# Second token group's v units by seven block products with transposes, ahead of the attention

## The chip, the cores and the metric

The kernel runs on one core of a Trainium2 chip. The time is in device microseconds (us), the median of the runs shown; the profile is one further execution on the same kind of chip. The engines are named as in the profile: PE (TensorE, matmuls), PEld (its weight loads), DVE (VectorE), ACT (ScalarE), POOL (GpSimd) and SP (SyncE, which here only issues DMAs).

## The reference

One encoder layer over 1280 tokens (1024 of a prompt, 256 of a sample), model width 2048, everything float32:

```
hn   = rmsnorm(x, norm_w)
proj = einsum('btd,dp->btp', hn, w_in)        # 2048 -> 9232 columns
na_q, na_k, na_v, na_g, ml_qk, ml_v, ml_o, ml_z, ml_gp = split(proj)
att  = neighbourhood_attention(na_q, na_k, na_v, na_rpb)   # 8 heads of 128
att  = att * silu(na_g)
qk   = silu(centred_depthwise_conv(ml_qk)); mq, mk = split(qk)
h    = bidirectional_mlstm(mq, mk, ml_v, gates)            # 4 heads of 256
mem  = rmsnorm(h) * sigmoid(ml_o) * silu(ml_z)
y    = rmsnorm(x + concat(att, mem) @ w_out)
```

The change touches only how the columns na_v and ml_v of `proj` are computed for some of the tokens.

## The kernel before

Every float32 operand of a large matmul is split into a high and a low half (ACT copies the high half, DVE subtracts to get the low one), and each product is the sum of three matmuls. The 1280 tokens go in two groups: 768 (group one, `GA`) and 512 (group two, `GB`). The projection's columns go in units of 256: `n1` counts columns in steps of 128, q from 0, k from 8, g from 16, conv (ml_qk) from 24, o from 40, z from 48, and eight v units from `NCH` = 56, of which v units 0 to 3 serve attention heads two by two and v units 4 to 7 serve one mLSTM head each.

The program has four stages.

- **Group one** (`first_tiles`, `unit_vg`, `pair_a`): every unit by seven products of half-size blocks in place of eight (a Strassen scheme). Four of its weight sums, `SUMS` = 6, 5, 7, 3, are written to DRAM (`sD`, line 590) for each unit in the table `SECOND`.
- **Group two, ahead of the attention**: v units 4 and 0 and one q unit plainly (`proj_v`, `proj_pair`), then each unit of `SECOND` by seven products (`pair_s`, matmuls of 256 columns, tiles named `S<n1>...`), reading the stored sums back. `finish_s` finishes a unit while the next one's products run.
- **The attention and the mLSTM** (`run` over two streams of steps; tiles `nas`, `nap` for the attention, `mls`, `mlp` for the mLSTM). The remaining units of group two are written in the program ahead of it, at lower priority, so that a planner with a simulated clock lays them between the attention's instructions on each engine: `proj_v` (tiles `pv`, `wsv`) for v units 1, 2, 3, 5, 6, 7, `proj_pair` (tiles `pc`, `ws`, `pco`) for nine pairs of q and conv columns and, last of all, eight pairs of o and z columns in `late_gate`. In this document these are called the fillers.
- **The output projection** (`product`, tiles `mb`, `mo`, `wo`, `po`): 14 block products. Its operand blocks `mb` are read back from DRAM by DMAs that POOL issues; their tiles lie in memory that the attention's pool (`att_ctx`) gives up.

A plain v unit is 4 token tiles x 16 slices of the model width x 3 matmuls = 192 matmuls of 256 columns; a plain pair is 96 matmuls of 512 columns; a unit by seven products is 7 x 8 x 3 = 168 matmuls of 256 columns.

All engines run their instructions in the order that the planner has set; an instruction waits for its semaphores and holds up what is behind it on its engine. So PE takes an attention matmul only where the order has it, and an engine can run ahead only as far as the tiles' buffers allow (for example one `npt` buffer, three `nst`, eight `hf`, five PSUM banks of tag "a").

Of the kernel before, what the change touches and what calls it, by code (L numbers as in the profile page):

```python
# [10 lines left out]
F32R = mybir.dt.float32r  # L11
# [3 lines left out]
P = 128  # L15
# [5 lines left out]
GA, GB = 768, 512  # L21
GSZ, GOF = (GA, GB), (0, GA)
NA_H, ML_H = 8, 4
EPS = 1e-6
NEG = -1.0e30
NCH = 56
# [3 lines left out]
NRA, NWS, NWT, NPC, NPO = 3, 8, 4, 5, 6  # L30
# [9 lines left out]
SECOND = (  # L40
    GT0, QK0 + 8, GT0 + 2, QK0, KT0, GT0 + 4, KT0 + 2, GT0 + 6, KT0 + 4,
    KT0 + 6,
)
LATE = (0, 2, 4, 6)
SUMS = (6, 5, 7, 3)

# [2 lines left out]
def kernel(  # L49
# [18 lines left out]
    V, S, G, PE, DM = nc.vector, nc.scalar, nc.gpsimd, nc.tensor, nc.sync  # L68
# [5 lines left out]
    def f(ap):  # L74
        return ap.bitcast(F32)

    def bank(tag, name):
        return ps.tile([P, 512], F32, tag=tag, name=name, bufs=3 if tag == "pr" else 5)
# [19 lines left out]
    ident = const.tile([P, P], F32, tag="ident", name="ident")  # L98
# [78 lines left out]
    def split(hi, lo, src, scale=None):  # L177
        if scale is None:
            S.copy(hi, src)  # L179
            return V.tensor_tensor(lo, src, f(hi), op=ALU.subtract)  # L180
        else:
            S.mul(hi, src, scale)
            return V.scalar_tensor_tensor(lo, src, scale, f(hi), op0=ALU.mult, op1=ALU.subtract)
# [30 lines left out]
    def store_qk(n, C, new, parts):  # L214
        hi, lo = new(F32R), new(F32)
        for c0, w, row in parts:
            cs = slice(c0, c0 + w)
            if row is None:
                split(hi[:, cs], lo[:, cs], C[:, cs])
            elif n < KT0:  # L220
                split(q_view(hi[:, cs]), q_view(lo[:, cs]), q_rows(C[:, cs]))
            else:
                split(k_view(hi[:, cs]), k_view(lo[:, cs]), k_rows(C[:, cs]))
        if n < KT0:
            store_q(n, (f(hi), lo), parts)
            return
        w = sum(w for _, w, _ in parts)
        t0 = 0 if w == GA else GA
        for z, t in enumerate((f(hi), lo)):
            DM.dma_start(kS[n - KT0][:, z, t0 : t0 + w], t[:, :w])  # L230
# [4 lines left out]
    def store_v(u, t0, o, src, scale=None):  # L235
        if u >= NA_H // 2:
            hi, lo = o[:, 0], o[:, 1]
        else:
            hi, lo = (o.rearrange("p a (j d) -> p (a j) d", j=2).rearrange(
                "p (j z) d -> p z j d", z=2)[:, z] for z in range(2))  # L240
            src = src.rearrange("p (j d) -> p j d", j=2)
        split(hi, lo, src, scale)
        flat = f(o).rearrange("p a d -> p (a d)")
        if u >= NA_H // 2 or t0 >= TP:
            DM.dma_start(vS[u][t0 : t0 + P], flat)
            return
        dst = vS[u][t0 // 256 * 256 : t0 // 256 * 256 + 256].rearrange("(c r) x -> r c x", r=4)
        for r in range(2):
            DM.dma_start(dst[t0 % 256 // 64 + r], flat[64 * r : 64 * r + 64])
# [397 lines left out]
    wb, xp0 = pools  # L647
# [9 lines left out]
    def po(name):  # L657
        return wb.tile([P, 520], F32, tag="po", name=name, bufs=NPO)
# [15 lines left out]
    def conv_b(o, ct):  # L674
        cv = po(f"pcv{ct}")
        yield from conv_taps(cv, o, ct, 516, 0)
        hi = wb.tile([P, 520], F32R, tag="po", name=f"pch{ct}", bufs=NPO)
        store_conv(ct, cv, hi, o, ((0, 258, GA - 2), (260, 516, TP)))
# [700 lines left out]
    def pair_s(n1, tag, bg):  # L1379
# [63 lines left out]
        for o, c in zip(Cn, ((c0, c1), (c2, c3))):  # L1443
# [3 lines left out]
            else:  # L1447
                out_scaled(o[:, :GB], o[:, :GB], rbs[1], n1)
        return finish_s(n1, Cn)

    def finish_s(n1, Cn):
        for j, o in enumerate(Cn):
            if QK0 <= n1 < OT0:
                ct = n1 - QK0 + j
                DM.dma_start(o[:, 0:4], qb[ct])
                for z in (260, 518):
                    G.memset(o[:, z : z + 2], 0.0)
                yield from conv_b(o, ct)
                continue
            o = o[:, :GB]  # L1460
            if n1 < GT0:
                store_qk(
                    n1 + j, o,
                    lambda dt: wb.tile([P, 520], dt, tag="po", name=f"S{n1}_{j}_{dt}", bufs=NPO),
                    PARTS_B,
                )
                yield
                continue
            if OT0 <= n1 < ZT0:
                S.activation(o, o, AF.Tanh, scale=0.5)  # L1470
            elif n1 >= GT0:
                th = po(f"S{n1}th{j}")[:, :GB]
                S.activation(th, o, AF.Tanh, scale=0.5)
                V.scalar_tensor_tensor(o, th, 1.0, o, op0=ALU.add, op1=ALU.mult)
            DM.dma_start(pT[n1 + j][:, GA:], o)
            yield
# [16 lines left out]
    for i in range(ML_H):  # L1493
        for u in (("v", 4 + i), QK0 + 8 + 2 * i, QK0 + 2 * i, ("v", i), QT0 + 2 * i, KT0 + 2 * i):
            if isinstance(u, tuple):
                if i:
                    proj_v(u[1], X)
            elif u not in SECOND and u != QT0:
                proj_pair(u, X)
# [368 lines left out]
```

## Time and profile before

| | us |
|---|---|
| median of 3 runs | 2542.15 (2541.53 to 2543.43) |
| span of the profiled execution | 2540.0 |
| PE busy | 2523.1 |
| DVE busy | 1980.9 |
| ACT busy | 1348.3 |
| POOL busy | 597.7 |

The profiled execution's own time is its span of 2540.0 us, 2.15 us under the median of the runs. "Busy" on PE counts a matmul from its start to its modelled end, and neighbours overlap, so a busy PE is not a PE at its peak; the number of matmuls in a stretch of time tells more. Group one ends at about 1089 us, the units of `SECOND` at 1362 us, the last attention matmul at 2100 us, and the output projection starts at 2143 us.

### The profile page before, as it was taken

The numbers are of one execution on the slowest core, as the hardware profiler recorded it, in microseconds if no ns is written. First come the engines' busy times: TensorE is split into PE (matmuls) and PEld (weight loads), VectorE is DVE, ScalarE is ACT, GpSimd is POOL, SyncE is SP. The second block draws the span as 40 slices with busy tenths as digits, with TensorE's granted clock in tenths as the row PEclk, the third lists the DMA queues.
The fourth block names the chain that finished last, engine by engine and source line by source line (L and its number), as shares of the span: only waits on it lengthen the run. The fifth ranks groups of instructions, "written<-read, shape, count | busy, mean of one in ns | idle before, by whom it ended". The sixth has DMA issues, their size and how long they took to land.

```text
span 2540.0 us, 44864 instructions
## 1 busy us (share of the span) xinstructions
PE 2523.1 (99%) x15197; PEld 2363.7 (93%) x15197; DVE 1980.9 (78%) x4034; ACT 1348.3 (53%) x3052; POOL 597.7 (24%) x883
## 2 busy tenths in 40 slices
PE   9999999999999999999999999999999999999998
PEld 9999999999999999999999899899998888888887
DVE  8787878898879798898875676775875665889696
ACT  8644455444444444475655666666665653344445
POOL 0553555544444454400000011010100103000002
PEclk9999999999999999999999999999999999999999
DMA  6563464546434342467778878878977849546327
GB/s 218 171 206 122 140 215 146 183 130 201 152 112 130 100 140 89 151 229 221 230 249 279 263 265 290 284 252 274 300 219 246 287 125 355 198 146 208 95 87 257
DMA packets 308189, 505.67 MB, mean 199 GB/s; under 512 B 49040, under 2 KB 195000, under 8 KB 307960
## 3 DMA queue, kind: packets, MB, share of 16 engines
q1 hardware_dynamic: 304856, 490.75, 60.0%
q0 software_dynamic: 2960, 11.80, 1.2%
q8 instruction: 120, 1.97, 0.3%
q14 instruction: 109, 0.89, 0.1%
q10 hardware_dynamic: 144, 0.26, 0.0%
HBM read 374.18 MB, written 128.52 MB: 198 GB/s over the span
## 4 chain that ended last, share of the span: by engine, by line
PE 87%; DMA 2%; DVE 2%; issue 0%; ACT 0%; POOL 0%; SPq 0%; POOLq 0%; ACTq 0%; DVEq 0%
PE pc L694 16%; PE po L1684 15%; PE pv L777 5%; PE A22b L288 1%; PE A44b L288 1%; PE A14b L288 1%; PE A18b L288 1%; PE A10b L288 1%; PE A48b L288 1%; PE A52b L288 1%; PE A50b L288 1%; PE A42b L288 1%; PE A20b L288 1%; PE A16b L288 1%; PE A12b L288 1%; PE A70b L288 1%
## 5 line engine op out<-in xcount | busy, mean ns | idle before, releaser
L1684 PE MATMUL po<-wo,mo 128*128 128x512 f32 (+1 forms) x1620 | 374.2, 392 | 0.0
L1684 PEld LDWEIGHTS po<-wo,mo 128*128 128x128 f32 x1620 | 303.3, 188 | 70.1
L180 DVE TENSOR_TENSOR ws<-wr,ws 128x512 fp32r<-128x512 f32 x144 | 97.9, 690 | 40.4 <-ACT ws L179 38.0
L179 ACT CAST ws<-wr 128x512 fp32r<-128x512 f32 x144 | 87.5, 617 | 64.9 <-PE pc L694 56.3
L179 ACT CAST mo<-mb 128x640 fp32r<-128x640 f32 x72 | 52.0, 726 | 108.8 <-PE po L1684 96.2
L120 POOL TENSOR_SCALAR rs<-rs 128x1 f32<-128x1 f32 x9 | 4.2, 468 | 370.4 <-DVE rs L1637 367.2
L180 DVE TENSOR_TENSOR mo<-mb,mo 128x640 fp32r<-128x640 f32 x72 | 58.4, 817 | 32.2 <-ACT mo L179 32.1
L1605 DVE TENSOR_TENSOR y<-y,po 128x512 f32<-128x512 f32 x89 | 57.2, 680 | 13.5 <-PE po L1684 13.3
L179 ACT CAST mo<-ms 128x640 fp32r<-128x640 f32 x40 | 28.9, 725 | 51.9 <-PE po L1684 30.6
L180 DVE TENSOR_TENSOR wsv<-wr_v,wsv 128x512 fp32r<-128x512 f32 x64 | 44.6, 702 | 12.5 <-ACT wsv L179 12.2
L179 ACT CAST wsv<-wr_v 128x512 fp32r<-128x512 f32 x64 | 38.9, 616 | 23.1 <-PE pv L777 13.5
L430 DVE SCALAR_TENSOR_TENSOR pcv<-pco,cw_sb,pcv 128x516 f32<-128x516 f32 x48 | 36.1, 753 | 7.7 <-ACT pcv L424 7.7
L180 DVE TENSOR_TENSOR mo<-ms,mo 128x640 fp32r<-128x640 f32 x40 | 32.7, 816 | 10.7 <-ACT mo L179 10.7
L1118 POOL MEMSET mls_0v<- 128x2 f32 x4 | 0.4, 102 | 163.4 <-DVE S_dt.float L180 139.0
L1619 ACT ACTIVATE jk<-y 128x512 f32<-128x512 f32 x39 | 24.5, 629 | 26.0 <-DVE y L1605 25.6
L133 ACT ACTIVATE xq<-xq 128x1024 f32<-128x1024 f32 x20 | 21.2, 1062 | 29.6 <-DMA xq<-in_xtok_dram 25.1
L288 PE MATMUL fb<-xg,fw 128*128 128x384 f32 x192 | 34.7, 335 | 0.2 <-ACT xg L186 0.2
L288 PEld LDWEIGHTS fb<-xg,fw 128*128 128x128 f32 x192 | 33.3, 188 | 0.5 <-ACT xg L186 0.5
L1568 DVE TENSOR_TENSOR ms<-mb,mb 128x640 f32<-128x640 f32 x40 | 32.6, 815 | 0.0
L815 DVE CUSTOM_DVE_ANT_0 nap_0st<-nap_0s,nap_0bt 128x384 f32<-128x384 f32 x32 | 17.7, 553 | 17.4 <-PE nap_0s L810 6.7
L818 ACT ACTIVATE nap_0st<-nap_0st,nap_0sm 128x384 f32<-128x384 f32 x32 | 19.7, 616 | 21.4 <-DVE nap_0sm L815 21.4
L265 DVE TENSOR_TENSOR pco<-pc,rstdb 128x512 f32<-128x512 f32 x28 | 19.1, 685 | 14.2 <-PE pc L694 14.0
(2770 smaller groups left out, 8507.2 us busy)
## 6 DMA issues: line engine op xcount, KB each, us to landing
wr<-in_w_in_dram SPq DMA_DIRECT2D x72, 512.0 KB, 4.9
wr_v<-in_w_in_dram SPq DMA_DIRECT2D x32, 512.0 KB, 4.6
wb<-in_w_o_dram SPq DMA_DIRECT2D x48, 256.0 KB, 3.4
xq<-in_xtok_dram SPq DMA_DIRECT2D x20, 512.0 KB, 4.3
mb<-mx POOLq DMA_DIRECT2D x32, 320.0 KB, 7.8
y<-in_xtok_dram SPq DMA_DIRECT2D x35, 256.0 KB, 5.3
wr_wp<-in_w_o_dram SPq DMA_DIRECT2D x16, 512.0 KB, 6.5
vS<-vo SPq DMA_DIRECT2D x24, 256.0 KB, 5.5
```

Source lines behind the costliest of these rows:

```text
L133: S.activation(raw, raw, AF.Square, accum_out=ssq[g][:, t, q : q + 1])
L179: S.copy(hi, src)
L180: return V.tensor_tensor(lo, src, f(hi), op=ALU.subtract)
L288: PE.matmul(o, w(a_), x(b_), start=first and m == 0, stop=last and m == 2)
L430: V.scalar_tensor_tensor(dst[:, a:n], src[:, a + j - pad : n + j - pad], cw_sb[:, ct, j : j + 1], dst[:, a:n], op0=ALU.mult, op1=ALU.add,)
L694: PE.matmul(pb[j], t[j][:, wi, c : c + P], xs[xi], start=first and m == 0, stop=last and m == 2,)
L777: PE.matmul(outs[tt], xs[:, tt * P : (tt + 1) * P], t[:, wi, q * w : (q + 1) * w], start=first and m == 0 and (gates or tt % 2 == 0), stop ...
L818: S.activation(st, st, AF.Exp, bias=sm[:, 0:1], scale=-1.0, accum_out=sm[:, 2:3])
L1568: V.tensor_tensor(t, x, y_, op=op)
L1605: V.tensor_tensor(Y[p, q, tt], Y[p, q, tt], bk, op=op)
L1619: S.activation(jk, Y[p, q, tt], AF.Square, accum_out=ss[t][:, c : c + 1])
L1684: PE.matmul(bk[tt] if o is None else o, m[xi][:, tt * P : (tt + 1) * P], w[wi][:, cs], start=first and kk == 0 and j == 0, stop=last and j ...
```

## The change

`SECOND` gets six more entries, the v units 5, 1, 6, 2, 7, 3. With that their sums are stored in group one (16 DMAs of 128 KB each per unit), they run by `pair_s` ahead of the attention, and they are left out of the fillers. Since `pair_s` gives columns by tokens and the attention wants tokens by columns, `finish_s` gets a branch for v units: two PE transposes of 128x128 per token tile into a PSUM bank (eight per unit), then the split and the store as before, but without the scale, which `pair_s` has applied to the whole unit.

```
 SECOND = (
     GT0, QK0 + 8, GT0 + 2, QK0, KT0, GT0 + 4, KT0 + 2, GT0 + 6, KT0 + 4,
     KT0 + 6,
-)
+) + tuple(NCH + 2 * u for u in (5, 1, 6, 2, 7, 3))
...
     def finish_s(n1, Cn):
+        if n1 >= NCH:
+            for tt in range(GB // P):
+                b = bank("a", f"S{n1}v{tt}")
+                for j in range(2):
+                    PE.transpose(b[:, j * P : (j + 1) * P], Cn[j][:, tt * P : (tt + 1) * P], ident)
+                o = wb.tile([P, 520], F32R, tag="po", name=f"S{n1}o{tt}", bufs=NPO)
+                o = o[:, :512].rearrange("p (a d) -> p a d", a=2)
+                store_v((n1 - NCH) // 2, GA + tt * P, o, b[:, :256])
+                if tt % 2:
+                    yield
+            return
...
             if isinstance(u, tuple):
-                if i:
+                if NCH + 2 * u[1] not in SECOND and u[1] not in (0, NA_H // 2):
                     proj_v(u[1], X)
```

The order on PE where the ten old units of `SECOND` end (S14 is the last of them, `xs` their operand sums). Before, the first filler v unit follows:

```order
L1416 MATMUL S14by<-xs_5_13893,S14s_16468 128x256 x3
L1416 MATMUL S14by<-xs_6_13908,S14s_16468 128x256 x3
L1416 MATMUL S14by<-xs_7_13923,S14s_16468 128x256 x3
L777 MATMUL pv_0_16506<-wsv_0_0_16510,x_0h 128x256 x2
L777 MATMUL pv_0_16506<-wsv_0_0_16510,x_0l 128x256
L777 MATMUL pv_0_16506<-wsv_0_0_16510,x_1h 128x256 x2
```

Now v unit 5 (S66) follows by seven products, and its transposes stand among the products of the next unit (S58):

```order
L1416 MATMUL S58by<-x_15l,S58s_16917 128x256
L1416 MATMUL S58by<-x_15h,S58s_16917 128x256 x2
L1456 MATMUL S66v_16933<-ident,S66c_16609 128x128
L1456 MATMUL S66v_16933<-ident,S66c_16610 128x128
L1456 MATMUL S66v_16940<-ident,S66c_16609 128x128
L1456 MATMUL S66v_16940<-ident,S66c_16610 128x128
L1416 MATMUL S58bx<-xs_0_13935,S58s_16949 128x256 x3
```

What moved: six units stand ahead of the first attention matmul that stood among the attention's.

The order on PE at the attention's end, before: the last attention matmuls (nap_3o of head 7, lines 932 and 938) have fillers (`pc`) ahead of them and behind them, and the output projection (`po`) comes after two more pairs.

```order
L694 MATMUL pc_0_26238<-x_8l,ws_00_26242 128x512
L694 MATMUL pc_0_26238<-x_8h,ws_00_26242 128x512 x2
L932 MATMUL nap_3o<-nap_3pt,nap_3v 128x256 x6
L938 MATMUL nap_3o<-nap_3pt,nap_3v 128x128 x2
L694 MATMUL pc_0_26238<-x_9l,ws_00_26242 128x512
L694 MATMUL pc_0_26238<-x_9h,ws_00_26242 128x512 x2
```

Now the last filler matmul stands ahead of the mLSTM's state step 2 of its last head (mlp3a2kv):

```order
L694 MATMUL pc_1_26651<-x_15h,ws_31_26753 128x512 x2
L694 MATMUL pc_1_26651<-x_15l,ws_31_26753 128x512
L1132 MATMUL mlp3a2kv_24412<-mlp3a2v,mlp3a2w_24406 128x258 x2
L1132 MATMUL mlp3a2kv_24420<-mlp3a2v,mlp3a2w_24406 128x258 x2
L1132 MATMUL mlp3a2kv_24412<-mlp3a2v,mlp3a2w_24406 128x258
```

and the attention's last rows on PE are followed at once by the output projection:

```order
L1303 MATMUL mlp_3tp<-ident,mlp_3hs 128x128 x4
L923 MATMUL nap_3o<-nap_3pt,nap_3v 128x2x128 x2
L932 MATMUL nap_3o<-nap_3pt,nap_3v 128x256 x6
L938 MATMUL nap_3o<-nap_3pt,nap_3v 128x128 x2
L1695 MATMUL po_0_0_26896<-wo_2_0_26906,mo_2_0_26903 128x512 x3
L1695 MATMUL po_0_1_26897<-wo_2_0_26906,mo_2_0_26903 128x512 x3
```

What moved: no filler is left on PE behind mlp3a2kv, where about a fifth of the attention's matmuls still stand, and none between the attention and the output projection.

## The prediction

> **What bounds the kernel now.** I read the page's busy shares and slices first, then the chain that ended last, then the list of PE's waits, and last the stretches of time that the change touches.
>
> ```profile
> span 2540.0 us, 44864 instructions
> ...
> PE 2523.1 (99%) x15197; PEld 2363.7 (93%) x15197; DVE 1980.9 (78%) x4034; ACT 1348.3 (53%) x3052; POOL 597.7 (24%) x883
> ...
> PE   9999999999999999999999999999999999999998
> ...
> PE 87%; DMA 2%; DVE 2%; issue 0%; ACT 0%; POOL 0%; SPq 0%; POOLq 0%; ACTq 0%; DVEq 0%
> ```
>
> PE is busy in every slice and carries the chain. So work taken from PE shortens the kernel, as long as PE still has something to do at each moment. In the list of waits PE has only two inside the attention:
>
> ```profile
> PE nas_0s L810 <- DMA nas4qk<-qS: 0.8, 1, 0.8
> ...
> PE nap_0s L810 <- DMA nap3qk<-kS: 0.6, 1, 0.6
> ```
>
> That is because the fillers stand between the attention's matmuls. The stretches, from the view of busy time by windows (after the length: PE, PEld, DVE, ACT, POOL busy with counts, granted clock, DMA share, GB/s):
>
> ```profile
> 317.50:381.00 63.50, 63.50 (x371) 63.12 (x370) 50.37 (x103) 32.22 (x81) 34.23 (x36) 1.00 0.68 215
> 825.50:889.00 63.50, 63.50 (x369) 63.46 (x368) 45.69 (x90) 29.38 (x69) 26.60 (x36) 1.00 0.31 100
> 1166.00:1362.00 196.00, 196.00 (x1703) 195.50 (x1702) 153.77 (x298) 116.43 (x225) 0.39 (x6) 1.00 0.73 229
> 1362.10:1372.50 10.40, 10.40 (x91) 10.40 (x90) 5.00 (x10) 2.91 (x7) 0.36 (x9) 1.00 0.91 284
> 1386.00:1940.00 554.00, 552.48 (x3640) 505.87 (x3639) 392.03 (x1081) 343.12 (x861) 56.19 (x207) 1.00 0.83 271
> 1830.00:1866.00 36.00, 36.00 (x303) 36.00 (x302) 32.41 (x92) 27.23 (x68) 3.37 (x16) 1.00 0.76 240
> 1939.70:2103.00 163.30, 163.30 (x928) 142.38 (x927) 106.72 (x287) 91.64 (x223) 10.31 (x32) 1.00 0.64 206
> 2105.00:2140.00 35.00, 35.00 (x153) 28.32 (x152) 14.40 (x22) 11.10 (x18) 17.17 (x32) 1.00 1.01 382
> ```
>
> The first two are group one with and without stored sums, the third is the ten units by seven products, the fourth a plain v unit alone, the fifth and seventh the attention with fillers, the sixth the last v unit beside it, the eighth fillers alone.
>
> **Part 1, what PE saves.** Ten units by seven products took 196 us with 1703 matmuls, of which 1680 are products; less about 2 us for the other 23 that is 19.4 us a unit. A plain v unit is 192 matmuls: at 10.40/91 = 0.114 us alone it takes 21.9 us, at 36.00/303 = 0.119 us beside the attention 22.8 us. Five of the six and most of the sixth lie beside it, so I take 22.8 and keep 21.9 for the range. The saving is 6 x 3.4 = 20.4 us (at least 6 x 2.5 = 15).
>
> The 48 transposes come back on PE. Three attention transposes in a row take this:
>
> ```profile
> 2040.45 0.49 PE L827 MATMUL nap_0t<-ident,nap_0st 128*128 128x128 f32 x3
> ...
> L476 PE MATMUL A60v<-ident,A60c x12: 270/272/272, 448.5 to 471.5; 128*128 128x128 f32 x12
> ```
>
> One lasts 0.27 us, so the other two add (0.49 - 0.27)/2 = 0.11 us each: 48 x 0.11 = 5.3 us (at most 48 x 0.27 = 13 if none overlaps). Net PE saving 20.4 - 5.3 = **15 us** (2 to 15 by the bounds).
>
> **Part 2, what is hidden.** The stored sums add 96 DMAs on SP's queue in group one, each about 0.32 us to issue, 31 us over six units:
>
> ```profile
> L590 SPq DMA_DIRECT2D sD<-A10t x16: 319/320/537, 313.5 to 343.4; - x16
> ```
>
> The stretch 317.5 to 381 holds two such units (A10 and A12): PE passed 371 matmuls there, 369 in the stretch without stored sums, with the DMA share at 0.68 against 0.31. I take 0; if that cover failed, the weight loads behind the stores on SP would be late, and I allow 0 to 6 us. A v unit by seven products has 14 splits of 512 columns where the plain one has 8, and some evictions more on DVE; in the stretch of the old ten units DVE is at 153.77/196 = 0.78 and PE does not wait, so 0 again. Its reads (3.5 MB a unit, as for the old ten) come at their 0.73 DMA share.
>
> **Part 3, what is uncovered.** The order on PE shows attention and fillers mixed as before, about one to two by matmul columns, only that there are six fillers fewer, so the fillers end early. Behind the last one stands the attention from mlp3a2kv on. In the trace of before that is what ran from 1939.7 us to the end of head 7, with these fillers in it (the windows view for tile ws, then pco; the columns are PE, PEld, DVE, ACT for the first and DVE, ACT, POOL for the second):
>
> ```profile
> 1939.70:2103.00 163.30, 117.24 (x456) 82.10 (x456) 26.11 (x39) 23.89 (x39) 1.00 0.64 206
> 1939.70:2103.00 163.30, 17.47 (x26) 5.87 (x10) 0.00 (x0) 1.00 0.64 206
> ```
>
> 456 of the 928 matmuls are fillers; at 35.00/153 = 0.229 us each (fillers alone) they are 104.3 us, so the attention's part of PE is 163.3 - 104.3 = 59.0 us. How long does this tail last with nothing else to run? DVE's own part is 106.72 - 26.11 - 17.47 = 63.1 us, ACT's 91.64 - 23.89 - 5.87 = 61.9 us: the tail can't be shorter than 63 us. If only PE's fillers were taken out and nothing moved up, it would stay 163 us. That it moves up is seen where one block follows another, on the one npt buffer (nap_0pt must be read by nap_0o before nap_1pt is written):
>
> ```profile
> 2024.21 0.55 DVE L830 TENSOR_TENSOR nap_0pt<-nap_1t,nap_0pt 128x384 fp32r<-128x384 f32 x1
> ...
> 2041.81 0.40 PE L923 MATMUL nap_0o<-nap_0pt,nap_0v 128*128 128x256 f32 x2
> ...
> 2047.18 0.33 PE L938 MATMUL nap_0o<-nap_0pt,nap_0v 128*128 128x128 f32 x2
> ...
> 2049.10 0.55 DVE L830 TENSOR_TENSOR nap_1pt<-nap_1t,nap_1pt 128x384 fp32r<-128x384 f32 x1
> ```
>
> nap_0pt was ready at 2024.8 and PE came to it at 2041.8: 17 of the 25 us between the two pt are PE's order, and they go. What then limits is DVE and ACT, in order, in turn with PE and the loads. I take DVE at the share that it has in this same stretch, 106.72/163.3 = 0.65: 63.1/0.65 = **97 us**. At the best share of the rows above, 32.41/36 = 0.90 from 1830 to 1866, it is 70 us. The loads agree: 206 GB/s x 163.3 us = 33.6 MB less the weights of 456/96 = 4.75 filler pairs, 2 MB each, is 24 MB, 63 us at 382 GB/s and 89 us at 271 GB/s. So PE idles 97 - 59 = **38 us** in the tail (4 to 104 by the ends).
>
> The way into the output projection is bare too:
>
> ```profile
> 2100.21 0.33 PE L938 MATMUL nap_3o<-nap_3pt,nap_3v 128*128 128x128 f32 x2
> ...
> 2102.61 0.32 SPq L951 DMA_DIRECT2D mx<-nap7o  x1
> ...
> 2106.42 4.00 POOL L1529 DMA_DIRECT2D mb<-mx  x7 [25.15 <-DMA mx<-pco]
> ...
> 2113.70 2.27 ACT L179 CAST mo<-mb 128x640 fp32r<-128x640 f32 x3 [3.38 <-DMA mb<-mx]
> 2114.46 2.37 DVE L180 TENSOR_TENSOR mo<-mb,mo 128x640 fp32r<-128x640 f32 x3 [3.42 <-ACT mo L179]
> ...
> 2142.95 2.25 PE L1684 MATMUL po<-wo,mo 128*128 128x512 f32 x9
> ```
>
> The first mb load waits for the memory of the attention's pool, hence for head 7's last store; behind it on POOL's queue are all other mb loads, and PE waits for the first split. From nap_3o's end (2100.54) to the first mo (2114.46 + 0.79 = 2115.25) are **14.7 us**. Before, fillers covered them up to 2143; now nothing does. I take 14.7 (12 if the load lands faster; 0 if the loads could start earlier, which the shared memory speaks against).
>
> **The sum.** -15 + 0 + 38 + 14.7 = +37.7 us against the profiled 2540.0 us: 2577.7, and 2.15 us more on the scale of the median: **2580 us**. The difference that a measurement of this kernel can tell from none is about 0.2%, 5 us.
>
> A rule that bears on this is in the Trainium skill, "TensorE: Matmul & The Clock Gate", Part 1 (the warmup mystery): after an idle window of about 3.4 us the array's clock drops to half, and it takes about as long a busy time to come back. It speaks against the change, since it makes an idling PE slower as well; by it the tail would be the third rival below, by the rows above the sum stands as it is.
>
> **Rivals.**
>
> 1. *The tail closes up and the gap is hidden: faster.* PE would run the tail's 59 us dense and the product phase would start at once; the end would be 2542 - 15 = 2527 us. For it: PE's order delays blocks by 17 us, so much was ready early. Against it: DVE needs 63 us for the tail, and with the 14.7 us gap even a dense tail gives only -0.3 us. It decides for "faster" only if tail and gap together leave PE idle less than 10 us. Chance 0.04.
> 2. *The tail runs at DVE's floor, the gap stays: no change.* 4 + 14.7 - 15 = +4, 2546 us. Tails up to 64 us give this. Chance 0.07.
> 3. *PE runs the tail at half rate.* The program's first 15 matmuls, of 384 columns, after an idle PE, show such a rate:
>
> ```profile
> 1.37 4.90 PE L342 MATMUL fb<-idle 128*128 128x384 f32 x15 [1.37 <-DVE idle L340]
> ```
>
> 4.90/15 = 0.327 us each, against 63.5/371 = 0.171 us in group one: 59 us become 113 us, and the tail lasts at least that: 113 - 59 + 14.7 - 15 = +54, 2596 us. For it: the tail's PE would be idle four tenths of the time. Against it: 38 us of idling spread over the nine attention blocks that are left there, each with three visits to PE, are gaps of about 1.4 us (an estimate), not one long one. Chance 0.13. (The page named above gives the rule for this.)
> 4. *The tail keeps its pace of before*, because the loads or the buffers set it: 104 + 14.7 - 15 = +104, 2646 us. Against it are the 17 us above. Chance 0.10.
>
> **How the numbers follow.** The likeliest case, a tail between 65 and 130 us (+6 to +71 us), has 0.66. The range runs from 2550 (a tail of about 67 us) to 2630 (a tail of about 147 us, which takes in the half rate); rival 1, most of rival 2 and rival 4 lie outside. The likeliest case's own range is 2548 to 2613. Slower by over 0.2%: 0.66 + 0.13 + 0.10 = 0.89; within 0.2%: 0.07; faster: 0.04.
>
> **What would show it.** The units S66 to S62 should take about 19.4 us each plus 0.9 us of transposes, with no PE wait, and group one should keep its end at 1089 us. The fillers should end near 2143 - 15 - 59 = 2069 us, and behind that PE's waits should name na and ml tiles, in slices of 5 to 6 tenths, for about 97 us. Then PE should wait some 15 us for the first mo, released by an mb load. The output projection should keep its 383 us. I am wrong in the main step if the tail is under 70 us, or if PE's waits appear already among the fillers, or if the order's end is not the trace's. It would also be wrong if group one slows by its stores.

## The result, and the profile after

The changed kernel takes 2616.4 us (median of 4 runs, 2615.0 to 2616.8), the kernel before 2541.8 us beside it on the same chip: a ratio of 1.029 (95% interval 1.028 to 1.031), 74.6 us slower. The profiled execution has a span of 2614.9 us, 74.9 us more than before. The page's lines that answer to those shown of before:

```profile
span 2614.9 us, 45132 instructions
...
PE 2537.2 (97%) x15101; PEld 2364.8 (90%) x15101; DVE 2023.6 (77%) x4112; ACT 1374.1 (53%) x3112; POOL 592.9 (23%) x883
...
PE   9999999999999999999999999999999966899998
...
PEclk9999999999999999999999999999999988999999
...
PE 73%; DMA 5%; DVE 2%; ACT 1%; issue 1%; POOL 1%; SPq 0%; POOLq 0%; DVEq 0%; ACTq 0%
```

PE has fewer instructions than before (15101 for 15197) and yet is busy for longer (2537.2 us for 2523.1): some of it runs slower. The two slices with a 6, and the 8 behind them, are new; the three lie at 2092 to 2288 us, on both sides of the attention's end (2190 us). The granted clock is below 9 tenths in the first two of them, and PE's share of the chain that ended last has fallen from 87% to 73%. PE's list of waits, which before had nothing over 0.8 us inside the attention or behind it, names the places:

```profile
PE po L1695 <- DVE mo L180: 21.5, 3, 14.3
PE nap_0s L810 <- DMA nap7qk<-kS: 6.0, 1, 6.0
PE mlp_1in L1132 <- DVE mlp_0zr L1317: 5.9, 1, 5.9
PE nap_0o L923 <- DVE nas6ot L870: 5.6, 1, 5.6
PE nap_0s L810 <- DMA nap0qk<-kS: 3.3, 1, 3.3
PE mlp0a2kv L1132 <- issue: 2.5, 1, 2.5
```

Their columns are the sum, the number and the longest. The first row is the way into the output projection (14.3 us) with a second stop behind it (6.6 us), the next three are the attention's tail, the last two the attention's start. The stages by the view of windows (length, then PE, PEld, DVE, ACT, POOL busy with counts, granted clock, DMA share, GB/s):

```profile
1364.00:1484.00 120.00, 120.00 (x1045) 119.87 (x1044) 84.30 (x149) 63.10 (x127) 0.00 (x0) 1.00 0.71 224
1486.00:1560.00 74.00, 68.17 (x356) 58.30 (x355) 44.05 (x108) 39.54 (x97) 7.11 (x37) 0.93 0.87 277
...
1560.00:2082.00 522.00, 520.34 (x2959) 453.85 (x2958) 366.01 (x1005) 311.20 (x777) 48.71 (x182) 1.00 0.80 260
2082.00:2190.50 108.50, 75.72 (x468) 67.10 (x466) 68.84 (x229) 63.26 (x178) 12.02 (x36) 0.87 0.69 226
...
2190.50:2204.80 14.30, 0.36 (x1) 0.36 (x2) 6.60 (x12) 4.98 (x8) 6.48 (x12) 0.50 0.75 267
2204.80:2234.80 30.00, 23.40 (x90) 18.47 (x89) 6.80 (x11) 6.23 (x10) 10.76 (x20) 0.84 1.03 389
```

These are the six v units by seven products; the attention's start; the attention with fillers; the tail, from the last filler to the attention's last matmul; the gap; and the first 30 us of the output projection. Put beside the same stages of before, whose ends are in the trace, they add up to the difference:

| stage | us |
|---|---|
| group one (ends at 1090.0 us for 1088.8) | +1.2 |
| from there to the attention's first matmul 122.0 us longer, six plain units beside the attention gone (6 x 23.05 = 138.3, an estimate from 192 matmuls at about 0.12 us) | -16.3 |
| attention's start to the last filler: 585.6 us, where 770.4 - 138.3 - 59.0 = 573.1 was to be expected | +12.5 |
| tail, 108.6 us for the 59.0 us that its matmuls took before | +49.6 |
| gap behind the attention | +14.4 |
| output projection, 401.6 us for 388.7 | +12.9 |
| behind it | +0.6 |
| sum | +74.9 |

Two of these numbers are shared out by an estimate: with the prediction's 22.8 us for a plain unit, 1.5 us move from the third row to the second (-14.8 and +11.0), and the 59.0 us stand in the third row and the fourth with opposite signs.

### The profile page after: what moved, and what is told of

It reads as the page before. It is cut to its first block, busy times and chain, and to the rows that moved or that the text cites. A ratio compares the mean times of both kernels' runs of the same rounds, so it can differ in the third digit from the quotient of the medians.

```text
span 2614.9 us, 45132 instructions
## 1 busy us (share of the span) xinstructions
PE 2537.2 (97%) x15101; PEld 2364.8 (90%) x15101; DVE 2023.6 (77%) x4112; ACT 1374.1 (53%) x3112; POOL 592.9 (23%) x883
## 4 chain that ended last, share of the span: by engine, by line
PE 73%; DMA 5%; DVE 2%; ACT 1%; issue 1%; POOL 1%; SPq 0%; POOLq 0%; DVEq 0%; ACTq 0%
PE po L1695 14%; PE pc L694 14%; PE A52b L288 1%; PE A48b L288 1%; PE A22b L288 1%; PE A18b L288 1%; PE A44b L288 1%; PE A46b L288 1%; PE A42b L288 1%; PE A20b L288 1%; PE A16b L288 1%; PE A70b L288 1%; PE A38b L288 1%; PE A50b L288 1%; PE A36b L288 1%
## 5 line engine op out<-in xcount | busy, mean ns | idle before, releaser
L1695 PE MATMUL po<-wo,mo 128*128 128x512 f32 (+1 forms) x1620 | 379.9, 396 | 21.5 <-DVE mo L180 21.5
L1630 ACT ACTIVATE jk<-y 128x512 f32<-128x512 f32 x39 | 24.5, 629 | 24.1 <-DVE y L1616 23.9
L179 ACT CAST wo<-T 128x512 fp32r<-128x512 f32 x32 | 19.8, 617 | 17.2 <-PE po L1695 17.2
L499 PE MATMUL vg<-vgs,xg 128*128 128x272 f32 x216 | 28.6, 287 | 0.0
L815 DVE CUSTOM_DVE_ANT_0 nap_0st<-nap_0s,nap_0bt 128x384 f32<-128x384 f32 x32 | 17.7, 552 | 13.2 <-PE nap_0s L810 11.4
L499 PEld LDWEIGHTS vg<-vgs,xg 128*128 128x128 f32 x216 | 27.6, 188 | 0.0
```

What stands on the lines that cost most here:

```text
L499: PE.matmul(banks[z, tt], xop(i, kk, xi)[:, tt * P : (tt + 1) * P], t[:, wi], start=kk == 0 and i in (1, 3) and m == 0, stop=kk == 7 and i ...
L1630: S.activation(jk, Y[p, q, tt], AF.Square, accum_out=ss[t][:, c : c + 1])
L1695: PE.matmul(bk[tt] if o is None else o, m[xi][:, tt * P : (tt + 1) * P], w[wi][:, cs], start=first and kk == 0 and j == 0, stop=last and j ...
```

## The experiments

All times are medians, and the kernel before took 2540.7 to 2542.1 us beside them. Each edit is one to the changed kernel. "Theory 1" is the prediction's: PE runs out of fillers before the attention ends, and what follows is bare. "Cover" is other work that PE has while the attention or the next stage would make it wait. Differences between two of these kernels that did not run side by side are good to about 1 us, by what the kernel before moved.

**One unit, four units, and six units twice.** Three kernels change only how many fillers there are.

```
# one unit
-) + tuple(NCH + 2 * u for u in (5, 1, 6, 2, 7, 3))
+) + tuple(NCH + 2 * u for u in (5,))
# four units
+) + tuple(NCH + 2 * u for u in (5, 1, 6, 2))
# six ahead, and the plain ones computed once more as fillers
-                if NCH + 2 * u[1] not in SECOND and u[1] not in (0, NA_H // 2):
+                if i:
```

> Only v unit 5 goes by seven products ahead of the attention; the other five stay plain beside it. Theory 1 (the time was lost because the fillers end before the attention): the order on PE still has 40 us of fillers behind the attention, so nothing is uncovered and only the saving shows, about 22.8 - 20.1 = 2.7 us: 2539 us (2536 to 2542). Theory 2 (each unit moved costs by itself, through its stores in group one, its transposes or the later start of the attention): a sixth of +75 us, 2554 us.

> Four v units (5, 1, 6, 2) by seven products ahead, two plain beside the attention. Theory 1: behind the last filler stand 27 us of attention matmuls, half of the 55 us of the full change: saving 9 to 11 us, idle and slow PE in the tail about 25 us, entry into the output projection bare as in the full change (14 us of waiting and 13 us more in the first product): 2542 - 10 + 25 + 27 = 2584 us (2574 to 2595). Theory 2: four sixths of +75, 2592 us. It tells little apart by itself; with the run of one unit it gives the shape, flat and then steep (theory 1) or a straight line (theory 2).

> All six v units by seven products ahead as in the full change, and computed plainly beside the attention a second time (the same values stored again), so that PE has 138 us more work than in the full change. Theory 1: the added matmuls lie where PE stood idle or slow; nothing of the attention is uncovered, the entry is covered; time of before plus the six units, 2542 + 122 = 2664 us (2655 to 2675), only about 48 us above the full change, and the output projection back at 389 us. Theory 2: the added work adds up, 2616 + 138 = 2754 us.

Measured: one unit 2539.8 us (ratio 0.999, 0.998 to 1.000), four units 2589.4 (1.018, 1.017 to 1.020), six units twice 2670.2 (1.050, 1.049 to 1.052). All three are as theory 1 has it; four units alone would fit theory 2 (2592 us) as well, the other two don't. With one unit the fillers still end 39.9 us behind the attention and the output projection follows without a gap, in 388.7 us. With four there is a tail of 48.8 us and a gap of 13.9. The third is the clearest: 138 us of useless PE work added to the changed kernel cost only 53.8 us, because the tail, the gap and the slow first product were gone. A cost for each moved unit would have made the row of one, four, six an even one; it is -2, +47, +75 us.

**The place without the form.** Here the six v units are computed plainly, in front of the block products.

```
-) + tuple(NCH + 2 * u for u in (5, 1, 6, 2, 7, 3))
+)
...
+    for u in (5, 1, 6, 2, 7, 3):
+        proj_v(u, X)
...
-                if NCH + 2 * u[1] not in SECOND and u[1] not in (0, NA_H // 2):
+                if False:
```

> The six v units stay plain but are moved ahead of the units by seven products, hence ahead of the attention: the move without the form (no stored sums, no transposes). Theory 1: the same tail and entry as in the full change, and each unit 22.4 us in place of 20.1: 2616 + 14 = 2630 us (2622 to 2640), fillers ending about 57 us of attention matmuls too early. If the form is what costs (theory 2), the time comes back to about 2545 us.

Measured: 2620.2 us (1.031, 1.030 to 1.032), 2 us below theory 1's range and far from theory 2's 2545. So it is the place that costs; stores and transposes are not needed for it. The block products end 12.4 us later than in the changed kernel (1495.8 for 1483.4), but 11.9 of that are won back between the attention's start and the last filler (573.6 us for 585.5). So something at the attention's start hurts the changed kernel and not this one.

**The attention's start.** The six v units come ahead of the ten old units.

```
-SECOND = (GT0, QK0 + 8, ..., KT0 + 6) + tuple(NCH + 2 * u for u in (5, 1, 6, 2, 7, 3))
+SECOND = tuple(NCH + 2 * u for u in (5, 1, 6, 2, 7, 3)) + (GT0, QK0 + 8, ..., KT0 + 6)
```

> The changed kernel with the six v units ahead of the ten old units of the second token group's block products instead of behind them; all else the same. Rival theory (the attention's start, some 12 us slower than before, pays for stores and transposes of v units that lie right ahead of it): with the old ten units last, as before, the start recovers most of the 12 us: 2606 us (2600 to 2611). Theory 1 (the loss is where fillers are missing, at the end; the slow start is a wait for the first head's loads that stands there anyway): 2616 us (2611 to 2621).

Measured: 2605.0 us (1.025, 1.024 to 1.027), 11.4 us under the changed kernel. The rival was right. The same window as above, in this kernel:

```profile
1486.00:1560.00 74.00, 74.00 (x387) 63.04 (x387) 49.97 (x118) 43.84 (x103) 5.41 (x25) 1.00 0.91 304
```

PE passes 387 matmuls there for 356 and does not wait. In the changed kernel it waits twice (the rows on nap0qk and on "issue" above, 5.8 us in all) and then runs slowly for a while, at a granted clock of 0.50 from 1517.4 to 1527.6 us:

```profile
1516.00:1526.00 10.00, 7.24 (x27) 6.02 (x28) 7.86 (x18) 6.76 (x17) 3.63 (x6) 0.57 0.67 227
```

That the order of the units is the cause is shown. How it acts was not taken apart. The load that PE waits for (nap0qk) stands on SP right behind five stores of the last v unit, but it is hardly late: it is issued 9.6 us after the attention's first matmul, 7.8 us in this kernel and 9.4 us in the kernel before. What differs more is PE, which is ready for it 17.0 us after that first matmul and comes to it only after 23.4 and 23.8 us in the other two.

**The way into the output projection.** The Z pair of the last `late_gate`, 23 us of PE work (96 matmuls of 512 columns; the expectation counts them as 192 of half the width), is held behind the attention's last product (`last_att` is the last matmul nap_3o of head 7).

```
+        with tc.issue_after(last_att[0]) if ch == LATE[-1] else ExitStack():
+            zs = proj_pair(ZT0 + ch, X, True)
-        for j, z_ in enumerate(proj_pair(ZT0 + ch, X, True)):
+        for j, z_ in enumerate(zs):
```

> The changed kernel, but the second half of the last late gate (the Z pair of columns, 192 matmuls at 0.12 us = 23 us of TensorE work) is held on TensorE behind the attention's last product instead of filling the attention. Theory 1 (the entry into the output projection is bare: a gap of 14.3 us, and a first product 13 us longer than before because it starts on a half clock and waits for weights): the 23 us now lie in the gap and cover it. From the runs with more and fewer fillers the attention ends 0.28 to 0.40 us sooner for each us of fillers taken out of it, so here 6 to 9 us sooner; first output product at about 2207, output phase 389 instead of 402: 2605 us (2599 to 2611). Rival (the longer first product comes from the transfers alone, whatever TensorE did before it): output phase stays at 400 to 402 and the time is 2618 (2614 to 2624).

Measured: 2599.1 us (1.023, 1.021 to 1.024), 17.3 us under the changed kernel. The timeline of PE at the place (start, length, engine and line, output and inputs, count, and in brackets the idle time before it and what ended it), the changed kernel first:

```profile
2204.44 23.76 PE L1695 MATMUL po<-wo,mo 128*128 128x512 f32 x90 [14.34 <-DVE mo L180]
2234.83 1.62 PE L1695 MATMUL po<-wo,mo 128*128 128x512 f32 x3 [6.63 <-DVE mo L180]
2236.97 25.40 PE L1695 MATMUL po<-wo,mo 128*128 128x512 f32 x101 [0.52 <-DVE mo L180]
```

```profile
2197.71 30.03 PE L1699 MATMUL po<-wo,mo 128*128 128x512 f32 x129
2228.64 15.56 PE L1699 MATMUL po<-wo,mo 128*128 128x512 f32 x66 [0.91 <-DVE y L1620]
2245.58 16.80 PE L1699 MATMUL po<-wo,mo 128*128 128x512 f32 x71 [1.38 <-ACT wo L179]
```

With cover the first 129 matmuls pass in one go; the output phase takes 391.6 us instead of 401.6, and there is no gap. So 24 of the 27 us (the 14.3 of the gap, and 10.0 of the 12.9 by which the output phase was longer) are the price of the bare entry. The held work keeps PE busy and also gives the loads 23 us more to land, so this run does not part the clock from the loads. The changed kernel's trace does: in its output phase PE stands for 7.2 us and is busy for 11.8 us at a granted clock of 0.50, which costs about half of that, 5.9 us (an estimate). The attention itself took 15.7 us less than in the changed kernel, twice what I had expected.

**The loads in the tail.** Eight T blocks and the first wb blocks of the second output product are held on SP behind the last v load of the attention. In the changed kernel they go out at 2066 to 2093 us, when the fillers have given up their x tiles.

```
+            with tc.issue_after(last_v[0]) if p == 0 else ExitStack():
                 b11 = w_block(0, n0, kk, nm)
                 t = T2[kk] = xslot(20 + kk, f"T2_{nm}")
                 DM.dma_start(t, w_o[n1, :, kk * 512 : (kk + 1) * 512])
```

> The changed kernel, but the loads of the second output product's weights (eight T blocks and the first wb blocks, 12 loads of 256 KB) are issued on SP behind the last v load of the attention's last head; in the changed kernel they go out at 2066 to 2093, as soon as the fillers have freed their buffers, among the attention's own loads. Theory 1a (the tail's long waits of 5.6 to 6.0 us are loads that land late because of these transfers, 3 MB or 8 us at 390 GB/s): the tail falls from 108.7 to 92 to 101 us and the time to 2604 (2598 to 2611). Rival 1b (the waits are those of the attention's own loads and of its chain, the output weights only fill time in which nothing else was wanted): tail 106 to 110, time 2616 (2611 to 2622).

Measured: 2607.5 us (1.026, 1.025 to 1.028), 8.9 us under the changed kernel; the tail is 101.0 us. Theory 1a, at the long end of its range. The wait of 5.6 us behind nas6ot has become one of 1.6 us in PE's list, the two other long ones are still there:

```profile
PE nap_0s L812 <- DMA nap7qk<-kS: 5.9, 1, 5.9
PE mlp_1in L1134 <- DVE mlp_0zr L1319: 4.4, 1, 4.4
```

So about a third of the tail's long waits is collision with the output weights. The wait on nap7qk is not: from 2098 to 2130 us SP issues only the attention's and the mLSTM's own loads and stores, and the DMA engines are at a share of 1.04 (2105.5 to 2123.9 us). What the third wait (mlp_0zr) comes from was not isolated.

**The second stop in the output phase.** The last eight mixer blocks are loaded later, by SP.

```
-    Aa = [mix_block(0, 0, kk) for kk in range(8)]
+    Aa = [None] * 8
...
+        if p == 0:
+            with tc.issue_after(last_load["ins"]):
+                Aa[:] = [mix_block(0, 0, kk, DM) for kk in range(8)]
```

> The changed kernel, but the last eight of the 32 mixer blocks (first needed by the third output product) are loaded by SP behind the second product's weights instead of by POOL with the other 24 right after the attention; 2.6 MB, or 6.7 us at 390 GB/s, leave the stretch of 2195 to 2234. Theory 1c (TensorE's second stop in the output phase, 6.6 us at 2235, is a weight block that lands late because the mixer blocks fill the transfers): the block lands 6 us sooner, the stop goes and with it most of the half clock behind it: 2608 us (2604 to 2611), output phase 391 to 395. Rival (the block is late because its issue on SP stands behind nine loads of y): no change, 2616 us (2613 to 2621).

Measured: 2617.1 us (1.030, 1.029 to 1.032), no change: theory 1c fails. The stop of 6.6 us became one of 3.2, and others came behind it (2.9 on an mo of ACT, 1.4 and 0.9 on DVE's); the output phase takes 403.3 us. So the mixer blocks alone are not the cause. The changed kernel's trace shows what the stop of 6.6 us waited for, though PE's list names an mo. SP's queue, then DVE's:

```profile
2201.66 12.38 SPq L1624 DMA_DIRECT2D y<-in_xtok_dram  x9
2215.88 4.78 SPq L1560 DMA_DIRECT2D wb<-in_w_o_dram  x3
...
2233.26 0.69 DVE L1592 TENSOR_TENSOR T<-T,wb 128x512 f32<-128x512 f32 x1 [16.74 <-DMA wb<-in_w_o_dram]
2233.87 0.82 DVE L180 TENSOR_TENSOR mo<-mb,mo 128x640 fp32r<-128x640 f32 x1
```

DVE stood for 16.7 us on a wb block that SP had issued behind nine loads of y, and the mo that PE wanted stood behind it on DVE. That fits the rival; an order with wb ahead of y was not tried.

**All three together, and the smaller doses.** The first kernel joins the three edits that helped. The others have two units behind the old ten; two units ahead of them with the Z pair held; and one unit ahead of them.

```
# all three: v units first, T and wb held, Z pair held
# two units
+) + tuple(NCH + 2 * u for u in (5, 1))
# two units first, Z pair held
+SECOND = tuple(NCH + 2 * u for u in (5, 1)) + (GT0, QK0 + 8, ..., KT0 + 6)
# one unit first
+SECOND = tuple(NCH + 2 * u for u in (5,)) + (GT0, QK0 + 8, ..., KT0 + 6)
```

> The changed kernel with three edits together: the six v units first among the block products, the second output product's weight loads held behind the attention's last v load, and the Z half of the last late gate held on TensorE behind the attention. Alone they gave 11.4, 8.9 and 17.3 us against the changed kernel's 2616.4. Theory 1 (three separate prices: start, collision, bare entry): they add up, less a little where two of them act on the same tail: 2579 us (2574 to 2588), still 37 us above the kernel before, which is then the price of the tail alone. Rival (they all shorten the same stretch, whose length the attention's own pace sets): 2594 us (2589 to 2600).

> Only the two v units 5 and 1 ahead as block products (behind the old ten), the other four as before. In the order of instructions the fillers then end with the attention: no tail, but nothing is left for the gap in front of the output projection. Theory 1 (the entry is a step of its own: gap 14 and first product 13 as soon as nothing is left behind the attention): 2542 - 2 x 3.4 + 27 = 2562 us (2555 to 2568). Rival (cost only by idle time in the tail): 2535 to 2546 us.

> Two v units (5 and 1) as block products ahead of the old ten, and the Z half of the last late gate, 23 us, held on TensorE behind the attention. Theory 1: the held work covers the entry, the first heads start unhindered, and two units save 2 x 3.4 us, against 0 to 12 us of idle time inside the attention, which now has 23 us less to fill it: 2540 us (2535 to 2547). Rival (the entry's price is not one of cover): 2562 us (2555 to 2568).

> Only v unit 5 ahead as block products, and first among them, so that the old ten stand right ahead of the attention as in the kernel before. Theory 1 (some 40 us of fillers are left behind the attention, so every us that TensorE saves reaches the end): 3.4 us saved against the kernel before, 2538.5 us (2537 to 2540.5), a little under the 2539.8 of the same unit behind the old ten. Rival (the saving is eaten by the transposes' and stores' work elsewhere): 2542 us (2540.5 to 2544).

Measured, all three together: 2594.0 us (1.021, 1.019 to 1.022). The rival was right, the gains don't add up: 22.5 us of 37.6. From its first matmul to its last the attention took these times (the last column is filler work that lies behind it):

| kernel | attention, us | PE's cover behind it, us |
|---|---|---|
| before | 727.9 | 42.6 |
| changed | 694.2 | none |
| v units first | 680.3 | none |
| T and wb held | 682.2 | none |
| Z pair held | 678.5 | 23.1 |
| all three | 672.7 | 23.3 |

It gets shorter as more is taken away that stands in its way, but not by the sum of the single gains. What sets the 673 us that are left was not isolated. In the last stretch of that kernel PE is still idle for a quarter of the time, at a low clock:

```profile
2060.00:2168.00 108.00, 79.25 (x469) 71.65 (x470) 68.73 (x225) 63.33 (x177) 11.85 (x36) 0.80 0.66 220
```

Two units: 2577.8 us (1.015, 1.013 to 1.016), above either expectation. In that trace the fillers end with the attention (2150.2 and 2149.9 us), so there is no tail, and yet 36.7 us are lost. 30.4 of them are the entry; the first two rows of PE's waits are its gap and a stop behind it:

```profile
PE po L1695 <- DMA wb<-in_w_o_dram: 15.6, 1, 15.6
PE po L1695 <- DVE mo L180: 9.7, 1, 9.7
```

The gap is 15.6 us, and the output phase takes 403.5 us, 14.8 more than before. The amount of fillers doesn't explain this, their place does: with one unit 40 us of them lie behind the attention; with two, which take away 23 us more, none do, and the attention has grown from 706.8 to 735.0 us, because the planner has put 176 more pair matmuls (pc) into it (1582 for 1406). The attention's start, which I had left out of the sum, has 5.0 us of idle time and a granted clock of 0.98 from 1405 to 1490 us. With two units first and the Z pair held it is 2549.8 us (1.0036, 1.0023 to 1.0050): 28 us are back and the output phase is 389.9 us, but the time is 2.8 us over the expectation's range. From the attention's first matmul to the last filler PE stands for 8.2 us:

```profile
1415.00:2149.50 734.50, 726.26 (x4500) 650.59 (x4499) 508.22 (x1383) 439.15 (x1097) 76.18 (x257) 1.00 0.80 261
```

That is about as much as without the held pair (7.9 us), but it lies elsewhere: the 5.0 us at the start are gone, and 4.2 us of it now come from 2100 us on.

One unit first: 2539.0 us (0.999, 0.998 to 1.000, 11 runs against 16). Its fillers end at 2138.4 us, 3.7 us sooner than before when counted from the end of group one, so the saving is there in that trace. It and the same unit behind the old ten (2539.8) are the versions that aren't slower; that they are faster is not shown, since both intervals reach 1.

## Why the prediction was right, and where it was not

The direction, the main mechanism (PE runs out of fillers, and tail and entry are bare) and the range (2550 to 2630) were right; the size was half, +38 for +75 us. The tail and the gap cost 64 us, for 53 in the sum; another 25 us came from two places that the sum had at nothing, the attention's start and the output projection. By the prediction's steps:

- **What PE saves, -15.** About right: -16.3 (-14.8 with a plain unit at 22.8 us). The units started 20.2 us apart and the six took 120.3 us, where 6 x 20.3 = 121.7 was to be expected.
- **What is hidden, 0.** Group one ended 1.2 us later with its 96 stores, so the cover held. But the step left out what stands behind the v units in the order: the attention's first loads. The attention's start lost 12.5 us, and putting the v units first gave 11.4 back. I had looked for cover in group one and in the block products only. One sign that I had named for being wrong, PE's waits among the fillers, showed here: two of them, 5.8 us.
- **The tail, 38 from 97 - 59.** The mis-sized term is the length, 97: it was 108.6, so the tail cost 49.6 (and the fillers ended at 2082 for 2069 us, about 12 of these by the slow start). I had counted only idle time. PE is idle for 108.5 - 75.7 = 32.8 us, less than I said, but its matmuls took 75.7 us instead of 59.0. Of the 16.7 us the clock makes some 10: PE was busy for 20.0 us at a granted 0.50, which at full clock would be half (an estimate); the rest was not taken apart. The clock falls during three stops of 5.6 to 6.0 us; holding T and wb shortened one of them to 1.6. The share of DVE that I used came out near, 68.84/108.5 = 0.63 for 0.65, but that is partly luck: in the kernel before PE's fillers set it, here single waits do, and nothing measured ties the one to the other.
- **The gap, 14.7.** 14.3, and the chain is the one that the prediction showed: nap7o's store, then mb's load, then the first mo.
- **The output projection keeps its time.** Wrong: +12.9 (401.6 us; before it was 388.7, not 383). This is the second place that the sum had at nothing. The same 42.6 us of fillers that hid the first mo had also hidden 32 mb loads and the weights behind them. Without it the first product starts at half clock and runs into a second stop of 6.6 us: 7.2 us of standing and about 6 us of slow clock.
- **Rival 3, half rate.** Partly so. The clock did fall to half, but around single stops of 5.6 us or more, not for the whole tail (0.87 in the mean); that the rival's 113 us for the tail is nearer to the 108.6 than the sum's 97 is not its mechanism's merit. I had argued against it with gaps of 1.4 us spread evenly, and most gaps are of that kind (23 of the tail's 26 waits are under 1.3 us). The three that aren't were enough. The Trainium skill, "TensorE: Matmul & The Clock Gate", Part 1, gives half a clock after an idle window of about 3.4 us and as long a busy time to recover; the trace agrees with both if they are counted on a grid of 3.41 us (below), but from PE's restart the way back took 5.2 to 9.4 us.
- **Rivals 1, 2 and 4** didn't come: a tail of 108.6 us lies between DVE's floor of 63 and the 163 of an unchanged pace.

How much of the slow clock's 10 us lies on the path that sets the end was not measured: no run kept PE warm in the tail.

## What to carry to other kernels

Fillers that stand behind and beside a chain with many small waits are worth more than the time that they take: here the 42.6 us behind it covered a gap of 14 us, the loads and the clock of the stage behind (13 to 15 us more), and those beside it every wait of the attention over 0.8 us. So ask of a saving in fillers how much cover is left at the chain's end, in the order that the planner makes of it: the first unit of six was worth 2 to 3 us at most, the second already cost some 38, since the new order left nothing behind the attention, and 28 of these came back with 23 us held there and the units moved to the front. Whether a thinner mixture of the fillers that are left, over the whole attention, would do better in the changed kernel was not tried. When work moves ahead of such a chain, look at both ends: which loads stand behind it on the queue, and which buffers come free early and send transfers in between.

## What the runs showed of the hardware

What a single stop of PE costs behind itself was not in my sum. Windows of 2 us behind the gap of 14.3 us (changed kernel):

```profile
2204.40:2206.40 2.00, 1.96 (x5) 1.59 (x6) 2.00 (x3) 0.00 (x0) 0.88 (x2) 0.50 1.01 292
2206.40:2208.40 2.00, 2.00 (x6) 1.59 (x5) 0.20 (x1) 0.00 (x0) 1.01 (x2) 0.50 1.00 395
2208.40:2210.40 2.00, 2.00 (x6) 1.58 (x5) 0.00 (x0) 0.00 (x0) 0.60 (x2) 0.53 1.02 410
2210.40:2212.40 2.00, 2.00 (x10) 1.61 (x10) 0.77 (x2) 1.25 (x2) 0.78 (x2) 1.00 1.06 404
```

For 6 us PE passes 5 to 6 matmuls in 2 us, then 10: about 3 us are lost (the first 90 matmuls took 23.76 us; at 30.03/129 = 0.233 us, as in the kernel with the Z pair held, they take 21.0). It is much the same behind a stop of 6 us in the tail (on nap7qk, ended at 2130 us), and behind the next one (2149.65 us) it took longer, in a stretch where PE kept stopping for a little:

```profile
2129.80:2131.80 2.00, 1.80 (x6) 1.84 (x7) 0.47 (x1) 0.00 (x0) 0.65 (x2) 0.50 1.05 387
2131.80:2133.80 2.00, 2.00 (x11) 1.90 (x10) 1.59 (x8) 1.79 (x7) 1.24 (x3) 0.50 1.05 389
2133.80:2135.80 2.00, 1.71 (x9) 1.50 (x8) 0.76 (x3) 2.00 (x8) 0.87 (x2) 0.66 1.01 336
...
2149.60:2158.40 8.80, 7.55 (x33) 7.25 (x34) 4.58 (x20) 4.61 (x13) 0.00 (x0) 0.50 0.24 78
```

When the clock changes, it keeps to a grid. Read in windows of 0.2 us, the changed kernel's granted clock falls to 0.50 at 2094.2, 2128.3, 2148.8, 2189.8 and 2230.7 us and is back at 1.00 at 2104.4, 2135.2, 2159.1, 2210.3 and 2241.0 us. Two of these places:

```profile
2094.00:2094.20 0.20, 0.00 (x0) 0.00 (x0) 0.00 (x0) 0.00 (x0) 0.00 (x0) 1.00 1.04 396
2094.20:2094.40 0.20, 0.00 (x0) 0.00 (x0) 0.00 (x0) 0.00 (x0) 0.00 (x0) 0.52 1.03 367
2104.20:2104.40 0.20, 0.20 (x2) 0.20 (x2) 0.00 (x0) 0.00 (x0) 0.00 (x0) 0.50 1.05 374
2104.40:2104.60 0.20, 0.20 (x4) 0.20 (x3) 0.00 (x0) 0.16 (x1) 0.00 (x0) 0.88 0.86 302
```

In order of time they are 10.2, 23.9, 6.8, 13.7, 10.2, 30.7, 20.5, 20.5 and 10.2 us apart, which is 3, 7, 2, 4, 3, 9, 6, 6 and 3 times 3.41 us. In the step of 3.41 us ahead of each fall PE was busy for 0 to 1.7 us, in the step ahead of each rise for all of it; steps with 2.2 us of work left a slow clock slow (2152.2 to 2155.7, 2234.2 to 2237.6 us). So what a stop costs depends on where it falls on this grid and on how dense PE's work is behind it: from PE's restart the clock stayed at 0.50 for 6.9, 5.2, 9.4, 5.8 and 6.1 us. A single long stop is not needed either: the fall at 2189.8 us came 0.3 us ahead of the long gap, in a stretch of short waits.

And the transfers: from 2210 to 2234 us, with the DMA share at 1.0 and 390 GB/s, a wb block of 256 KB took 17.1 us from issue to landing (median), where it takes 3.5 us over the whole program.
